# Four gate projections moved between the retention's steps, one search operation moved to GpSimd, and the retention's PSUM copies moved to ScalarE

## The chip, the cores and the metric

The kernel runs on one core of a Trainium2 chip. The metric is the device time of one execution in microseconds (us); lower is better. The core's engines run their own instruction streams in order and wait for one another through semaphores: PE (TensorE, matmuls; PEld is its weight load), DVE (VectorE), ACT (ScalarE), POOL (GpSimd) and SP (SyncE, here the queue that issues most DMAs).

## The reference, cut to what matters

The program is two layers of a hybrid decoder trunk for 1024 tokens of width 1024. The change lies in the first layer, whose input projection feeds two head groups:

```python
h = rms_norm(x, pre_norm[0])
(aq, ak, av, ag, iq, ik, iw, bq, bk, bv, bg) = split_columns(h @ w_in, EVEN_WIDTHS)
a = dsa_attention(aq, ak, av, iq, ik, iw)      # 256 best keys of each row, then softmax over those
a = a * jax.nn.silu(ag)                        # the selected-key gate, 512 columns
r = head_group_norm(retention(rotary(bq), rotary(bk) * 64 ** -0.5, bv))   # 8 chunks of 128, a state carried along
r = r * jax.nn.silu(bg)
x = x + rms_norm(concatenate([a, r]) @ w_out, post_norm[0])
```

`dsa_attention` finds for each query row the 256 keys with the highest index score. `retention` works chunk by chunk: the product inside the chunk, plus the state from the earlier chunks. Every projection is computed to float32 accuracy from a high and a low part, as three matmuls (low x high, high x low, high x high).

## The kernel before

**Search.** For the rows' blocks 2 to 7, `emit_threshold` (L521) finds the 256th score of every row by bisection over the score's upper 15 and lower 16 bits: 31 rounds, each of two chains of three blocks. In a chain, `count` counts the keys below the candidate, on ACT for blocks 7, 6 and 3 (L516) and on DVE for 2, 5 and 4 (L519). Then three operations on 128x3 numbers form the next candidate: `alt` (L535, the next lower candidate, which needs only the old one), `flag` (L536, compares the counts) and `cand` (L537, picks). All three are on DVE. Masks follow (`emit_mask`, L594 to L606).

**Retention.** `retention(p)`, for p = 0 and 1, handles two heads each. It loads weights, projects q and k (`pbqk`, turned by `rope_pairs`, L639 to L644, on DVE straight from PSUM), transposes them (`btq`, `btk`), projects v (`pbv`, copied out by ACT, L693), and then goes through 8 chunk steps: scores `bs`, `bsT` (L717, DVE), a state `bstate`, the output `bo`, and in each step 12 matmuls of its own gate `pbg`. The output leaves PSUM through DVE (L752, 128x256), followed by the statistics (L755, L756) and, later, the normalization (L770).

**Gates.** `gate_t` makes x times a sigmoid from a PSUM tile: a tanh on ACT (L622) and one operation on DVE (L623), both reading PSUM. `A_gate(p)` loads 128 columns of weights and computes two PSUM tiles `pag` of 8 steps (24 matmuls of 128x512) each, then writes the gate out to DRAM; it is read back transposed by head when the attention is combined. It has one call for each p from 0 to 3: 64 steps, 192 matmuls in all.

**Staging.** The search and both retentions are emitted together. Then come A_v(0), A_gate(0), A_qk(0), with the rest of retention 1 and the masks woven in, and then the attention units `units_A(0)` to `units_A(3)`, into whose steps a fill of further projections is spread evenly: 48, 80, 48 and 16 steps. The order on each engine is then set by the tile framework's scheduler from what it expects of the program as emitted, with data dependences and buffers kept.

**Buffers.** PSUM tiles of the tag `pj` (`pbqk`, `pbv`, `pbg`, `pag`, `pav`, `paq`, `pak`) share 2 buffers; so a third tile waits until the first is read out. High and low weight tiles (`whi`, `wlo`) have 6 buffers each, raw ones 4. `split_hl` (L244) makes them: a cast (on ACT, L248, or on POOL, L250), then the low part on POOL (L251). In the units, POOL also prepares the padded queries `zq` (L417) that the score matmuls L412 read.

Of the kernel before, what the change touches and what calls it, by code (L numbers as in the profile page):

```python
# [21 lines left out]
P = 128  # L22
# [123 lines left out]
def tile_hybrid_decoder(ctx: ExitStack, tc, x, positions, pre_norm, post_norm, w_in_even, w_out_even, w_in_odd,  # L146
# [374 lines left out]
    def emit_threshold():  # L521
# [4 lines left out]
        def bisect(bits, unsigned):  # L526
            for g in range(len(CHAINS)):
                V.memset(cand[:, cs_[g]], 2.0 ** (bits - 1) - 0.5)
            for b in range(bits - 1, -1, -1):
                for g, chain in enumerate(CHAINS):  # L530
                    s = cs_[g]
                    for q in chain:
                        c = col[q]
                        count(q, keys[q].bitcast(U16) if unsigned else keys[q], cand[:, c:c + 1], cnt[:, c:c + 1])
                    V.tensor_scalar(alt[:, s], cand[:, s], 2.0 ** (b - 1), None, op0=ALU.subtract)  # L535
                    V.tensor_tensor(flag[:, s], cnt[:, s], need[:, s], op=ALU.is_le)  # L536
                    V.scalar_tensor_tensor(cand[:, s], flag[:, s], 2.0 ** b, alt[:, s], op0=ALU.mult, op1=ALU.add)  # L537
# [96 lines left out]
    def rope_pairs(dst, src, tmp, cos, sin, nsin, half):  # L634
# [9 lines left out]
        V.tensor_tensor(dst, t1, t2, op=ALU.add)  # L644


    new_keys()
# [4 lines left out]
    def retention(p):  # L652
# [72 lines left out]
        for n in range(NB):  # L725
# [25 lines left out]
            rr = r[n // 4][:, n % 4, :]  # L751
            V.tensor_copy(rr.rearrange("p (h t) -> p h t", t=P), po[:, :, 0:P])  # L752
            st6 = small("bst", (P, 2, 6))
# [33 lines left out]

    def until(gen, val):
        for z in gen:
            if z == val:  # L790
                return

    until(B[0], 2)
    for k in range(20):
        if k >= 3:
            next(B[0], 0)
        next(B[1], 0)
    drain(B[0])
    until(B[1], 2)
    if dbg and upto == 3:  # L800
# [138 lines left out]

    def A_gate(p):  # L940
        w = load_w(w_in_even[0], [(AG + P * p, P)], "wag", hi_eng=G)
        for half in range(2):
            pp = pst("pag", "pj")
            yield from proj_t(pp, w, hT, 0, P, half)
            gate_out(pp, p * P, half)


# [92 lines left out]
    todo = chain(*(emit_mask(q) for q in (6, 7, 4, 5, 2, 3)))  # L1040
    for i, _ in enumerate(chain(A_v(0), A_gate(0), A_qk(0))):
        if i % 4 == 3 and i >= 12:
# [4 lines left out]
    outE = OutProj(w_out_even[0], pg1, pg2, 4, pg_raw=pg2)  # L1047
    fill = chain(A_qk(1), A_gate(1), A_v(2), A_qk(2), A_gate(2), A_qk(3), A_gate(3))
    pipe.run(units_A(0), islice(fill, 48), 48)
    pipe.run(units_A(1), islice(fill, 80), 80)  # L1050
    pipe.run(units_A(2), fill, 48)
    pipe.run(units_A(3), outE.first(2), 16)
# [422 lines left out]
```

## Time and profile before

| | us |
|---|---|
| median of 3 runs | 1304.21 (1302.02 to 1307.22) |
| the profiled execution | 1303.41 |
| its span in the trace | 1301.6 |
| PE busy | 1246.0 (96%) |
| PEld busy | 1029.2 (79%) |
| DVE busy | 800.5 (62%) |
| ACT busy | 682.6 (52%) |
| POOL busy | 411.5 (32%) |

Busy times are of the whole span; stages differ. In the trace the search runs from about 94 to 257 us, the retentions from about 60 to 271, the masks to 302, the attention units from about 330 to 600. A PE that is "busy" is not at its peak rate; the profile also gives the clock that the throttle granted it in a stretch.

### The profile page before, as it was taken

The numbers are of one execution on the slowest core, as the hardware profiler recorded it, in microseconds if no ns is written. First come the engines' busy times: TensorE is split into PE (matmuls) and PEld (weight loads), VectorE is DVE, ScalarE is ACT, GpSimd is POOL, SyncE is SP. The second block draws the span as 40 slices with busy tenths as digits, with TensorE's granted clock in tenths as the row PEclk, the third lists the DMA queues.
The fourth block names the chain that finished last, engine by engine and source line by source line (L and its number), as shares of the span: only waits on it lengthen the run. The fifth ranks groups of instructions, "written<-read, shape, count | busy, mean of one in ns | idle before, by whom it ended". The sixth has DMA issues, their size and how long they took to land.

```text
span 1301.6 us, 20092 instructions
## 1 busy us (share of the span) xinstructions
PE 1246.0 (96%) x7138; PEld 1029.2 (79%) x7138; DVE 800.5 (62%) x2020; ACT 682.6 (52%) x1510; POOL 411.5 (32%) x626
## 2 busy tenths in 40 slices
PE   7999989999999999889999999999999899999998
PEld 4788778798779877667887888889888777777786
DVE  6499999994654436484433344533654888887522
ACT  5578759602532424454545454554655677776421
POOL 4302232245251241444331233212322520435330
PEclk9999999999999999899999999999999999999999
DMA  5201111114121131225441113121322420232531
GB/s 192 57 25 34 33 34 57 34 26 121 29 71 32 34 89 40 79 89 184 148 121 42 49 49 90 58 60 42 122 65 89 110 53 30 75 97 66 187 125 65
DMA packets 92052, 97.70 MB, mean 75 GB/s; under 512 B 8118, under 2 KB 74448, under 8 KB 91952
## 3 DMA queue, kind: packets, MB, share of 16 engines
q1 hardware_dynamic: 87696, 82.39, 20.8%
q0 software_dynamic: 3968, 12.99, 3.6%
q8 instruction: 56, 0.92, 0.3%
q10 hardware_dynamic: 288, 1.05, 0.2%
q14 instruction: 44, 0.36, 0.1%
HBM read 68.74 MB, written 24.77 MB: 72 GB/s over the span
## 4 chain that ended last, share of the span: by engine, by line
PE 75%; DVE 13%; issue 4%; ACT 4%; POOL 4%; DMA 0%; POOLq 0%; DVEq 0%; ACTq 0%
PE tp L309 6%; PE bank L1009 5%; PE So L847 4%; PE So L848 4%; PE So L849 4%; DVE tj L519 3%; PE S L412 3%; PE S L411 3%; PE co L1176 2%; PE S L1419 1%; PE pav L301 1%; PE pav L303 1%; PE pav L302 1%; PE S L1421 1%; PE S L1420 1%
## 5 line engine op out<-in xcount | busy, mean ns | idle before, releaser
L1026 ACT ACTIVATE ae<-ae,nmx 128x128 f32<-128x128 f32 (+7 forms) x128 | 99.2, 776 | 90.1 <-DVE nmx L1024 89.6
L516 ACT ACTIVATE aj<-keys,tk_cand 128x1024 bf16<-128x1024 int16 (+5 forms) x96 | 93.2, 971 | 37.9 <-DVE tk_cand L537 14.9
L309 PE MATMUL tp<-cs,ae 128*128 128x128 f32 x576 | 89.3, 284 | 5.4 <-DVE pT L995 3.7
L309 PEld LDWEIGHTS tp<-cs,ae 128*128 128x128 f32 x576 | 68.7, 144 | 28.3 <-issue 9.3
L847 PE MATMUL So<-woh,mixl 128*128 128x512 f32 x224 | 87.7, 391 | 0.0
L849 PE MATMUL So<-woh,mixh 128*128 128x512 f32 x224 | 87.5, 391 | 0.0
L848 PE MATMUL So<-wol,mixh 128*128 128x512 f32 x224 | 87.5, 390 | 0.0
L1024 DVE CUSTOM_DVE_ANT_0 ce<-S,cmask 128x128 f32<-128x128 f32 (+7 forms) x64 | 48.2, 754 | 54.2 <-PE S L412 53.6
L519 DVE TENSOR_SCALAR_CACHE_REDUCE tj<-keys,tk_cand 128x384 bf16<-128x384 int16 (+5 forms) x96 | 79.9, 833 | 1.3
L1026 ACT ACTIVATE ce<-ce,nmx 128x128 f32<-128x128 f32 (+7 forms) x64 | 49.7, 776 | 53.0 <-DVE nmx L1024 52.7
L993 ACT COPY pT<-tp 128x384 f32<-128x384 f32 (+1 forms) x80 | 43.0, 538 | 54.4 <-PE tp L309 47.7
L995 DVE COPY pT<-tp 128x512 f32<-128x512 f32 (+1 forms) x80 | 50.7, 633 | 25.7 <-PE tp L309 22.8
L417 POOL CAST zq<-cqs 64x128 fp32r<-64x128 f32 x64 | 19.4, 304 | 146.9 <-PE S L412 143.3
L417 POOL CAST zq<-aqs 64x128 fp32r<-64x128 f32 x64 | 20.2, 316 | 129.7 <-PE S L412 127.1
L973 DVE TENSOR_SCALAR ae<-ae,ars 128x128 f32<-128x128 f32 (+7 forms) x96 | 58.4, 609 | 2.2
L1024 DVE CUSTOM_DVE_ANT_0 ae<-S,cmask,nrq 128x128 f32<-128x128 f32 (+3 forms) x64 | 51.4, 812 | 10.1 <-PE S L1421 8.3
L251 POOL TENSOR_TENSOR mixl<-mixr,mixh 128x512 fp32r<-128x512 f32 x32 | 41.5, 1306 | 35.3 <-ACT mixh L248 33.6
L412 PE MATMUL S<-akl,zq 128*128 128x512 f32 (+2 forms) x96 | 34.0, 365 | 17.2 <-POOL zq L417 17.2
L847 PEld LDWEIGHTS So<-woh,mixl 128*128 128x128 f32 x224 | 42.1, 188 | 9.3 <-issue 0.8
L848 PEld LDWEIGHTS So<-wol,mixh 128*128 128x128 f32 x224 | 42.1, 188 | 8.6
L849 PEld LDWEIGHTS So<-woh,mixh 128*128 128x128 f32 x224 | 42.1, 188 | 8.5
L329 ACT ACTIVATE junk<-So 128x512 bf16<-128x512 f32 x24 | 14.2, 593 | 56.0 <-PE So L849 42.2
(427 smaller groups left out, 4067.9 us busy)
## 6 DMA issues: line engine op xcount, KB each, us to landing
mixr<-mixT SPq DMA_DIRECT2D x32, 256.0 KB, 3.2
gT<-gate SPq DMA_DIRECT2D x24, 256.0 KB, 2.1
waqkr<-in_w_in_even_dram SPq DMA_DIRECT2D x32, 128.0 KB, 2.5
gin<-gT SPq DMA_DIRECT2D x32, 128.0 KB, 2.4
mixT<-gin SPq DMA_DIRECT2D x32, 128.0 KB, 1.8
wor<-in_w_out_even_dram SPq DMA_DIRECT2D x8, 512.0 KB, 4.0
xr<-in_x_dram POOLq DMA_DIRECT2D x8, 512.0 KB, 3.9
x1d<-xr SPq DMA_DIRECT2D x8, 512.0 KB, 3.3
```

The source lines that it names most:

```text
L309: nc.tensor.transpose(dst[:, k * P:(k + 1) * P], s, ident)
L412: nc.tensor.matmul(S[:, c:c + w], b, kl[:, c:c + w], start=False, stop=True)
L516: A.activation(aj[:, 0:n], src, AF.Sign, scale=-1.0, bias=edge, accum_out=dst)
L519: V.tensor_scalar(aj[:, 0:n], src, edge, None, op0=ALU.is_lt, op1=ALU.add, accum_out=dst)
L847: nc.tensor.matmul(dst, ml[k][:, bs], hi, start=(k == 0), stop=False)
L848: nc.tensor.matmul(dst, mh[k][:, bs], lo, start=False, stop=False)
L849: nc.tensor.matmul(dst, mh[k][:, bs], hi, start=False, stop=(k == kc - 1))
L973: V.tensor_scalar(e, e, rs, None, op0=ALU.mult)
L995: V.tensor_copy(pts[m][:, r, 0:n], tp[:, 0:n])
L1009: nc.tensor.matmul(bank[hp, o:o + wd], vp[:, kb, hp], pT[:, h, c:c + wd], start=(n == 0 or j == 0 and n == 1), stop=(n == len(jobs) - 1 or ...
L1024: V.tensor_tensor_reduce(out=e[:, 0:n], in0=S[:, 0:n], in1=mask, scale=scale, scalar=3.4e38, op0=ALU.add, op1=ALU.min, accum_out=nmx)
L1026: A.activation(e[:, 0:n], e[:, 0:n], AF.Exp, scale=-1.0, bias=nmx, accum_out=rsum)
```

## The change

Three things are done. `alt` goes from DVE to GpSimd. The retention's output copy goes from DVE to ScalarE. And `A_gate` is defined before the retention, loads its weights 128 columns wide (two raw tiles of four row blocks in place of four half-used tiles of two), and its 64 steps are drained between the steps of the retentions (`until` and the loop of 20), where they were before in front of A_qk(0) (16 steps) and in the fills of units 0, 1 and 2 (16 steps each).

```diff
@@ emit_threshold
-                    V.tensor_scalar(alt[:, s], cand[:, s], 2.0 ** (b - 1), None, op0=ALU.subtract)
+                    G.tensor_scalar(alt[:, s], cand[:, s], 2.0 ** (b - 1), None, op0=ALU.subtract)
@@ ahead of retention; the old A_gate, behind A_v, is deleted
+    def A_gate(p):
+        w = load_w(w_in_even[0], [(AG + P * p, P)], "wag", width=P, hi_eng=G)
+        for half in range(2):
+            pp = pst("pag", "pj")
+            yield from proj_t(pp, w, hT, 0, P, half)
+            gate_out(pp, p * P, half)
@@ retention, chunk step
-            V.tensor_copy(rr.rearrange("p (h t) -> p h t", t=P), po[:, :, 0:P])
+            A.copy(rr.rearrange("p (h t) -> p h t", t=P), po[:, :, 0:P])
@@ behind B = [retention(p) for p in range(2)]
-    def until(gen, val):
+    gates = chain(*(A_gate(p) for p in range(4)))
+
+    def until(gen, val, steps):
         for z in gen:
+            drain(islice(gates, steps))
             if z == val:
                 return
 
-    until(B[0], 2)
+    until(B[0], 2, 1)
     for k in range(20):
         if k >= 3:
             next(B[0], 0)
         next(B[1], 0)
+        drain(islice(gates, 2))
     drain(B[0])
-    until(B[1], 2)
+    until(B[1], 2, 2)
+    drain(gates)
@@ behind emit_threshold
-    for i, _ in enumerate(chain(A_v(0), A_gate(0), A_qk(0))):
+    for i, _ in enumerate(chain(A_v(0), A_qk(0))):
@@
-    fill = chain(A_qk(1), A_gate(1), A_v(2), A_qk(2), A_gate(2), A_qk(3), A_gate(3))
-    pipe.run(units_A(0), islice(fill, 48), 48)
-    pipe.run(units_A(1), islice(fill, 80), 80)
-    pipe.run(units_A(2), fill, 48)
+    fill = chain(A_qk(1), A_v(2), A_qk(2), A_qk(3))
+    pipe.run(units_A(0), islice(fill, 32), 32)
+    pipe.run(units_A(1), islice(fill, 64), 64)
+    pipe.run(units_A(2), fill, 32)
```

In the changed file the retention's lines have numbers that are 7 higher (L717 is L724 there, L755 is L762).

The first place is VectorE's stream in the chunk steps of retention 0, in the middle of the search. Before:

```order
L535 TENSOR_SCALAR tk_alt<-tk_cand 128x3
L519 TENSOR_SCALAR tj_795,tk_cnt<-keys_793,tk_cand 128x768
L535 TENSOR_SCALAR tk_alt<-tk_cand 128x3
L519 TENSOR_SCALAR tj_795,tk_cnt<-keys_793,tk_cand 128x640
L752 COPY br_1358<-bo_1457 128x256
L717 TENSOR_TENSOR bsT_1473<-bs_1470,cb_797 128x256
L755 BN_STATS bst_1465<-br_1358 128x6 x2
L756 BN_AGGR bmv_1360<-bst_1465 128x2
```

And the changed kernel's:

```order
L536 TENSOR_TENSOR tk_flag<-tk_cnt,tk_need 128x3
L537 SCALAR_TENSOR_TENSOR tk_cand<-tk_flag,tk_alt 128x3
L519 TENSOR_SCALAR tj_795,tk_cnt<-keys_793,tk_cand 128x768
L519 TENSOR_SCALAR tj_795,tk_cnt<-keys_793,tk_cand 128x640
L762 BN_STATS bst_1498<-br_1424 128x6 x2
L763 BN_AGGR bmv_1426<-bst_1498 128x2
L623 SCALAR_TENSOR_TENSOR bg_1427<-bg_1427,pbg_1443 128x512
L763 BN_AGGR bmv_1426<-bst_1498 128x2
L724 TENSOR_TENSOR bsT_1509<-bs_1506,cb_797 128x256
```

The lines L535 and L752 are gone from this stream, and the search's other operations stand closer together.

The second place is GpSimd's stream around the weights of retention 0's gate (`wbgl`), in the same part of the search. Before:

```order
L677 TENSOR_TENSOR bqk_839<-bqk_839,cb_797 128x4x128
L251 TENSOR_TENSOR wbgl_1343<-wbgr_1344,wbgh_1342 128x256 x2
L251 TENSOR_TENSOR wbgl_1351<-wbgr_1352,wbgh_1350 128x256 x2
L251 TENSOR_TENSOR wbqkl_1638<-wbqkr_1639,wbqkh_1637 128x256 x2
L251 TENSOR_TENSOR wbqkl_1647<-wbqkr_1648,wbqkh_1646 128x256 x2
```

And the changed kernel's:

```order
L535 TENSOR_SCALAR tk_alt<-tk_cand 128x3 x9
L251 TENSOR_TENSOR wbgl_1393<-wbgr_1394,wbgh_1392 128x256 x2
L251 TENSOR_TENSOR wbgl_1401<-wbgr_1402,wbgh_1400 128x256 x2
L251 TENSOR_TENSOR wbgl_1409<-wbgr_1410,wbgh_1408 128x256 x2
L250 CAST wagh_1623<-wagr_1625 128x128 x4
L251 TENSOR_TENSOR wbgl_1417<-wbgr_1418,wbgh_1416 128x256
L251 TENSOR_TENSOR wagl_1624<-wagr_1625,wagh_1623 128x128
L251 TENSOR_TENSOR wbgl_1417<-wbgr_1418,wbgh_1416 128x256
L251 TENSOR_TENSOR wagl_1624<-wagr_1625,wagh_1623 128x128 x3
L535 TENSOR_SCALAR tk_alt<-tk_cand 128x3 x6
```

The search's `alt` now stands in one queue with the splits of the weights, here nine of it ahead of a run of 16 splits and six behind.

The third place is TensorE's stream in a chunk step of retention 0. Before:

```order
L742 MATMUL bo_1457<-bstate_1426,bqx_837 128x128
L715 MATMUL bs_1470<-bqT_835,bkT_836 128x128 x2
L734 MATMUL bu_1475<-bv_1102,bqk_838 64x128 x2
L289 MATMUL pbg_1444<-hTh_129,wbgl_1343 128x512
L290 MATMUL pbg_1444<-hTl_137,wbgh_1342 128x512
```

And the changed kernel's:

```order
L749 MATMUL bo_1490<-bstate_1459,bqx_837 128x128
L289 MATMUL pag_1301<-hTh_130,wagl_907 128x512
L290 MATMUL pag_1301<-hTl_138,wagh_906 128x512
L291 MATMUL pag_1301<-hTh_130,wagh_906 128x512
L722 MATMUL bs_1506<-bqT_835,bkT_836 128x128 x2
L741 MATMUL bu_1511<-bv_1139,bqk_838 64x128 x2
```

One step of a gate, three matmuls, now stands in each chunk step, and its tile `pag` keeps one of the two `pj` buffers over eight such steps.

## Rows read from the trace of the kernel before

**Rows 1.** The page, part 1: busy time, share of span, instructions.

```profile
PE 1246.0 (96%) x7138; PEld 1029.2 (79%) x7138; DVE 800.5 (62%) x2020; ACT 682.6 (52%) x1510; POOL 411.5 (32%) x626
```

**Rows 2.** Busy times by stretch: length, engines, granted clock, DMA share, GB/s.

```profile
100.00:270.00 170.00, 161.18 (x1079) 138.66 (x1077) 161.44 (x564) 118.43 (x254) 48.89 (x58) 0.99 0.14 37
182.00:257.00 75.00, 69.63 (x488) 61.46 (x488) 72.12 (x262) 58.45 (x123) 17.40 (x23) 0.98 0.14 40
330.00:600.00 270.00, 249.82 (x1496) 202.55 (x1497) 151.09 (x356) 117.48 (x242) 88.42 (x173) 0.96 0.21 61
```

**Rows 3.** PE's waits, 100 to 270 us: total us, times, longest us.

```profile
PE btq L309 <- DVE bqk L644: 2.1, 1, 2.1
PE bo L740 <- DVE br L752: 1.7, 2, 1.3
PE pbv L301 <- DVE rp L643: 1.0, 1, 1.0
```

**Rows 4.** Stretch behind the wait at 193.25: columns as in rows 2.

```profile
193.80:197.20 3.40, 3.40 (x18) 3.40 (x17) 3.29 (x14) 3.30 (x7) 1.27 (x1) 0.50 0.02 5
```

**Rows 5.** DVE's groups by form, 94 to 258 us: busy us, mean ns, idle before.

```profile
L535 DVE TENSOR_SCALAR tk_alt<-tk_cand 128x3 f32<-128x3 f32 x60 | 11.0, 193 | 0.0
L770 DVE TENSOR_SCALAR br<-br,bmv,brs 128x128 f32<-128x128 f32 x21 | 6.0, 341 | 4.2 <-POOL brs L242 4.2
L755 DVE BATCH_NORM_STATS2 bst<-br 128x6 f32<-128x128 f32 x24 | 5.7, 280 | 0.0
L717 DVE TENSOR_TENSOR bsT<-bs,cb 128x256 f32<-128x256 f32 x14 | 5.7, 416 | 0.0
L752 DVE COPY br<-bo 128x256 f32<-128x256 f32 x12 | 5.0, 419 | 0.0
L639 DVE TENSOR_TENSOR rp<-pbqk,tabB 128x512 f32<-128x512 f32 x6 | 4.1, 681 | 0.0
L623 DVE SCALAR_TENSOR_TENSOR bg<-bg,pbg 128x512 f32<-128x512 f32 x6 | 4.0, 663 | 0.6 <-ACT bg L622 0.6
L642 DVE TENSOR_TENSOR rp<-pbqk,tabB 128x256 f32<-128x256 f32 x6 | 2.5, 412 | 0.0
```

**Rows 6.** DVE's timeline at two places: start us, us.

```profile
138.06 0.17 DVE L535 TENSOR_SCALAR tk_alt<-tk_cand 128x3 f32<-128x3 f32 x1
138.18 0.88 DVE L519 TENSOR_SCALAR_CACHE_REDUCE tj<-keys,tk_cand 128x640 bf16<-128x640 int16 x1
...
206.94 0.70 DVE L536 TENSOR_TENSOR tk_flag<-tk_cnt,tk_need 128x3 f32<-128x3 f32 x1
207.67 0.66 DVE L537 SCALAR_TENSOR_TENSOR tk_cand<-tk_flag,tk_alt 128x3 f32<-128x3 f32 x1
```

**Rows 7.** POOL's timeline beside the two later rows of that.

```profile
206.36 3.38 POOL L251 TENSOR_TENSOR wbgl<-wbgr,wbgh 128x256 fp32r<-128x256 f32 x4
```

**Rows 8.** POOL's waits, 100 to 270 us: total us, times, longest us.

```profile
POOL wbgl L251 <- ACT wbgh L248: 28.1, 2, 15.2
```

**Rows 9.** ACT's groups by form, 60 to 330 us: busy us, mean ns.

```profile
L516 ACT ACTIVATE aj<-keys,tk_cand 128x1024 bf16<-128x1024 int16 x16 | 18.4, 1150 | 11.8 <-DVE tk_cand L537 8.2 <-DVE tk_need L569 2.5 <-DVE tk_flag L536 0.5
...
L693 ACT COPY bv<-pbv 128x256 f32<-128x256 f32 x16 | 5.6, 351 | 0.0
L622 ACT ACTIVATE bg<-pbg 128x512 f32<-128x512 f32 x8 | 4.7, 584 | 15.4 <-PE pbg L291 15.4
```

**Rows 10.** Tile `pag` alone, the first gate's stretch: PE, PEld, DVE, ACT, clock.

```profile
294.00:307.00 13.00, 11.68 (x48) 8.81 (x48) 0.69 (x1) 0.60 (x1) 1.00 0.32 86
```

**Rows 11.** PE's largest wait from 328 to 600 us.

```profile
PE S L412 <- POOL zq L417: 17.2, 6, 5.9
```

**Rows 12.** PE's timeline where unit 2 begins.

```profile
477.00 0.53 PE L412 MATMUL S<-akl,zq 128*128 128x256 f32 x1 [2.55 <-POOL zq L417]
```

**Rows 13.** POOL's groups by form, 318 to 560 us: busy us, mean ns.

```profile
L251 POOL TENSOR_TENSOR wagl<-wagr,wagh 128x128 fp32r<-128x128 f32 x24 | 10.8, 468 | 0.0
...
L250 POOL CAST wagh<-wagr 128x128 fp32r<-128x128 f32 x24 | 6.4, 296 | 11.6 <-PE pak L291 10.7 <-POOL zq L417 0.9
```

More of the change, by code (lines that the diff above doesn't have):

```diff
@@ L938, in A_v @@
                 A.activation(vs[i][:, b:b + 2, :], pp.rearrange("p (b i c) -> p b i c", b=2, i=2)[:, :, i, :], AF.Copy, scale=0.5)
[L940 to L945, printed above, removed]
     def pair_units(p, front, vp, row, grow, pages, merge=False):
```

## The prediction

> **What bounds the kernel now.** I read the page's busy shares first: PE is busy for 1246.0 of 1301.6 us [rows 1], so no more than 55.6 us of the span is PE idle time, and a change that leaves the matmuls as they are can only win there or from the clock. Next I read busy times by stretch. From 100 to 270 us, where search and retentions run, PE is busy for 161.18 of 170 us and DVE for 161.44 of 170 [rows 2]: two engines are nearly full, and PE idles 8.8 us. From 330 to 600 us, the attention units, PE idles 270 - 249.8 = 20.2 us, while DVE is only busy for 151 of 270 [rows 2]. PE's waits in the first stretch name DVE: 2.1 us for the rope's sum, 1.7 for the output copy L752, 1.0 for the rope's PSUM reads [rows 3]. Behind the 2.1 us wait PE runs 3.4 us at a granted clock of 0.50, the lower of its two levels [rows 4], which costs half of that, 1.7 us. So the change works on the stretch where DVE makes PE wait, and what can be had there is 8.8 + 1.7 = 10.5 us.
>
> The sum is made against the profiled execution's 1303.41 us, 0.8 us under the median of the runs, 1304.21.
>
> **The matmuls that move.** The 192 matmuls of the gates stay as they are, 11.7 us for each of the four gates [rows 10], some 47 us in all. They leave the stretch ahead of the units and three fills and enter the retentions. By themselves they cost or win nothing. What they win is time: they give PE work on which DVE has little to do (one operation of 0.66 us a tile [rows 5]).
>
> **What DVE is relieved of.** In the built order, between the first and the last `cand` (L537), DVE loses 60 `alt`, 12 output copies, 6 `bsT` and 8 `bst` (five chunk steps of retention 1 now stand behind the search's end) and gains two operations of L623. An `alt` lasts 193 ns by its group [rows 5], but in the timeline the next operation starts 0.12 us after it [rows 6]; operations overlap, so I count 0.1: 6 us. The copies are 12 x 0.42 = 5.0 us, `bsT` 6 x 0.42 = 2.5, `bst` 8 x 0.28 = 2.2, and the gates take back 1.3 [rows 5]: together 14 us of about 160.
>
> It is not spread evenly. In the search's second half, which in before is 182 to 257 us, PE idles 75 - 69.6 = 5.4 us and DVE 2.9 [rows 2]. There the order loses 32 `alt` (3.2 us), 6 copies (2.5), 3 `bsT` (1.2) and 2 `bst` (0.6), but takes in three gate operations (2.0) and seven more normalizations of L770 (7 x 0.34 = 2.4) [rows 5]: net 3 us. Of the 5.4 us, 3 come back; of the 3.4 in the first half, where the other 11 us of relief lie, all. **Term 1: -6 us** (0 to -8.8). The slow stretch at 193 us goes if its wait falls to a part; I count half of 1.7: **-0.8** (0 to -1.7).
>
> **Copies on ACT.** 16 copies of 128x256 from PSUM, 0.35 us each by the row of the same shape [rows 9], 5.6 us; ACT is busy for 118 of 170 us [rows 2] and has room. A copy can stand behind a count of 1.15 us [rows 9], but it holds an output buffer of which there are two, so it is hidden by the next chunk step (12 matmuls of 0.24 us, 2.9 us, by [rows 10]). Zero; if that cover were gone, 16 x 0.5 = 8 us, which I hold unlikely.
>
> **The buffers of tag `pj`.** This is the change's price. A `pag` tile now lives over eight steps with other work between, and so the other projections have one buffer left in place of two. In before, a `pbqk` tile's readout has the whole next tile to hide behind, 48 matmuls. In the changed order it has only what stands between: mostly two or three gate steps, 6 to 9 matmuls, 1.5 to 2.2 us [rows 10], or one step, 0.7. The readout takes 0.68 + 0.41 + 0.41 = 1.5 us for the rope, 0.58 + 0.66 = 1.25 for a gate [rows 5, 9], 0.35 for a copy on ACT, and up to 1.15 of queue ahead [rows 9]. I count 28 such places. Each is between 0 (an idle engine) and about 0.5 (1.5 + 1.15 against 2.2); I take 0.15, nearer to zero, since DVE and ACT wait in order and mostly stand ready: **term 2: +4 us** (0 to +14). The trace of before has no interleaved tile; its 1.0 us of `pbv` behind the rope [rows 3] shows that even a wide cover can fail.
>
> On this the Trainium skill, Perfetto Trace Analysis, section Matmuls, speaks against the change: independent matmul groups should rotate through different PSUM banks, so that one group's readout overlaps the next one's matmuls. No run so far shows its price; taken at its word the 28 readouts would stand uncovered, and the sum would rise by 10 us, to 1313.
>
> **POOL's queue.** `alt` needs only the old candidate, so on POOL it runs beside the counts; its result is due a count later, 0.88 us or more [rows 6]. But POOL works in order, and the stretch's queue is full of weight splits that wait: `wbgl` alone for 28.1 us in two waits, up to 15.2 [rows 8], until PE lets go of weight buffers. In the changed order nine `alt` stand ahead of one run of 16 splits and six behind; the run lasts 8 x 0.85 (3.38 for four [rows 7]) + 4 x 0.30 + 4 x 0.47 [rows 13] = 9.8 us. If it starts late, `cand` waits for `alt`, everything on DVE stands behind `cand`, and PE behind the rope. Three or four such runs lie in the search. The scheduler has put the `alt` where they fit by its own plan, and DVE has 14 us less to do; I take **+2 us** (0 to +16).
>
> There is a second effect. At 206.94 `flag` and `cand`, 128x3, last 0.70 and 0.66 us [rows 6], beside a run of POOL splits from 206.36 [rows 7]. POOL is busy for 48.9 us of the stretch [rows 2]; it gains 32 gate splits (16 x 0.30 + 16 x 0.47 = 12.3 us [rows 13]) and 62 `alt`. If small DVE operations suffer in proportion, and some ten lost half a microsecond each in before, that is 5 x 12.3 / 48.9 = 1.3: **+1 us**.
>
> The Trainium skill, Perfetto Trace Analysis, section Optimizing Scalar/DVE Operations, says that GpSimd and DVE share a read port of SBUF, and that moving work between them might not help. The slow `flag` agrees with it. By that rule the 6 us of `alt` would not be won, and the sum would be 1307.
>
> **The units.** Fills of 48, 80 and 48 steps become 32, 64 and 32. Unit 3 runs with 16. PE's largest wait there is for `zq` on POOL, 17.2 us in 6 times [rows 11], where splits for the fill stand ahead of it. At unit 2, 4 casts and 4 splits of `wag` (4 x 0.30 + 4 x 0.47 = 3.1 us [rows 13]) leave POOL's run in front of `zq`, and one split of another weight takes their place; of the 2.55 us wait [rows 12] I let about 2 go. At unit 0 splits twice as wide come in for them, +1. Thinner fill can uncover softmax chains: DVE has 151 us for what becomes 250 - 35 = 215 of PE, still no bound. **Term 3: -1 us** (-4 to +5).
>
> **Sum:** -6 - 0.8 + 4 + 2 + 1 - 1 = -0.8, so 1302.6; I say **1302 us**, about no change.
>
> **The rivals.**
> - *The stretch becomes purely PE-bound* (faster). The readouts and `alt` hide, as DVE's relief of 14 us against 8.8 us of idle PE allows: -8.8 - 1.7 - 1 gives 1292. For it: all of PE's large waits in the stretch are for DVE. Against it: in the second half only 3 us are taken off DVE, and a buffer is taken away at the same time.
> - *POOL's queue holds the search* (slower). Three runs of 9.8 us, each holding `cand` by half, 15 us of DVE time, on an engine that was 95% busy; the relief of 14 us is eaten, PE stays as late as before, and the readouts' 4 us and some of the queue come on top: 1303.4 + 10 = 1313. It decides from about 13 us of DVE waiting for POOL on.
> - *Single buffer at full price*: 28 x 0.5 = 14 in place of 4 gives 1312.
> - *The move only shifts the loss* (the fills are missed in the units): +5 in place of -1, 1308, within no change. That the scheduler would put the gates back is excluded by the built order.
>
> **How the numbers follow.** A measurement of this kernel tells about 0.5%, 6.5 us, from no change. Chances: no change as forecast 0.44 (with 1308 and the 1307 of the shared port in it), the PE-bound stretch 0.30, slower 0.26 (POOL 0.15, buffers 0.11). The forecast's own range is 1297.7 to 1310. The range for 8 in 10 reaches from 1291, all of the idle and slow time gone, to 1315, just beyond the two slower cases.
>
> **What would show it.** Right: PE's idle time from 100 us to the end of retention 1 falls from 8.8 to between 5 and 10 with the waits now many and short, at the first matmul of `pbqk`, `pbv`, `pbg` and `pag`, for DVE's rope, L623 or ACT's copies; the wait for L752 is gone; DVE waits for `alt` a few times behind weight splits. The units' idle time stays near 20 us. Wrong: PE waits below 3 us in the stretch (the buffers cost nothing), waits of `cand` for `alt` of over 10 us, or units that differ by more than 5 us. What would upset the sum is a change of the granted clock elsewhere, as a slow stretch of 3.4 us costs 1.7.

## The result and the profile after

The changed kernel takes 1320.57 us (median of 4 runs, 1319.26 to 1322.71); the kernel before, on the same chip, 1305.51 us (4 runs). The ratio is 1.012 with a 95% interval of 1.0093 to 1.0148: some 15 us slower. The time lies above the predicted 1302 us and above the whole range, 1291 to 1315. The two profiled spans are 1320.9 and 1301.6 us, 19.3 us apart, so the profiled pair lies a little further apart than the medians (15.1 us).

The page's busy times of the changed kernel, beside [rows 1]:

```profile
PE 1256.1 (95%) x7138; PEld 1030.9 (78%) x7138; DVE 799.8 (61%) x1942; ACT 691.3 (52%) x1526; POOL 418.3 (32%) x688
```

PE does the same 7138 matmuls and is busy 10 us longer, which already says that part of the loss is a lower clock or wider spacing, not idle time alone. DVE has 78 instructions fewer and is off by 0.7 us only.

To place the loss, I cut both traces at the same points of the program: **R**, from the first matmul of retention 0 (`pbqk`) to the first `pav`, holds search and retentions; **U**, from there to the first matmul into the tile `So`, holds the attention units; then the rest. Busy times by stretch (length, engines, granted clock, DMA share, GB/s), of before:

```profile
62.10:270.80 208.70, 199.66 (x1327) 172.66 (x1325) 196.48 (x632) 148.30 (x302) 53.24 (x63) 0.99 0.14 37
270.80:597.20 326.40, 305.41 (x1841) 252.49 (x1840) 188.94 (x428) 126.70 (x261) 117.52 (x223) 0.97 0.22 64
597.20:1295.20 698.00, 686.33 (x3729) 566.94 (x3728) 377.01 (x881) 372.88 (x876) 215.51 (x302) 1.00 0.29 87
```

and of after:

```profile
62.00:326.80 264.80, 250.37 (x1517) 209.64 (x1516) 218.89 (x610) 160.64 (x327) 87.43 (x185) 0.98 0.17 47
326.80:616.90 290.10, 265.98 (x1649) 218.76 (x1648) 166.41 (x373) 123.30 (x254) 89.35 (x160) 0.95 0.19 56
616.90:1314.50 697.60, 686.39 (x3729) 566.65 (x3728) 376.50 (x881) 373.31 (x877) 215.96 (x302) 1.00 0.29 87
```

The rest is the same to 0.4 us. The gates' 192 matmuls left U and entered R; in before, counted from the start of each to the start of the next, they fill 45.2 us. Taking these 45.2 us along:

| part | before | after | moved work | net | of it idle PE | of it clock | left over |
|---|---|---|---|---|---|---|---|
| R | 208.7 | 264.8 | +45.2 | +10.9 | +5.4 | +3.4 | +2.1 |
| U | 326.4 | 290.1 | -45.2 | +8.9 | +3.1 | +5.1 | +0.7 |

Idle PE is length less PE's busy time (R 9.0 to 14.4, U 21.0 to 24.1 us). The clock's part is half the added time at the lower level (a granted clock of 0.50): 3.4 to 10.2 us in R, 20.5 to 30.7 us in U. It is a little too high where PE also idles in such a stretch, which then counts twice.

**R.** PE's waits in after (what PE waited for: us in total, times, longest):

```profile
PE pbv L301 <- DVE gate L623: 3.2, 1, 3.2
PE pbqk L301 <- DVE tk_flag L536: 2.7, 1, 2.7
PE pbv L301 <- DVE rp L643: 2.4, 2, 1.8
PE pag L289 <- DVE tk_flag L536: 2.1, 1, 2.1
PE pbqk L301 <- DVE tk_cand L537: 2.0, 1, 2.0
...
```

The waits of before for `btq` and `bo` [rows 3] and for `btr`, 5.3 us together, are gone. Every wait now stands at the first matmul of a projection that needs a `pj` buffer: 14.2 us in ten waits, against 2.5 us in three in before. Four of the ten, of 2.0 to 3.2 us, make 10.0 of the 14.2. Where the releaser reads `tk_flag` or `tk_cand`, the profile names the operation that happened to end last; in the stream of VectorE it is the rope's readout that holds the buffer (start, duration, line, operation):

```profile
102.19 0.61 DVE L519 TENSOR_SCALAR_CACHE_REDUCE tj<-keys,tk_cand 128x384 bf16<-128x384 int16 x1
...
103.19 1.01 DVE L519 TENSOR_SCALAR_CACHE_REDUCE tj<-keys,tk_cand 128x768 bf16<-128x768 int16 x1
...
104.25 0.88 DVE L519 TENSOR_SCALAR_CACHE_REDUCE tj<-keys,tk_cand 128x640 bf16<-128x640 int16 x1
...
105.05 0.69 DVE L639 TENSOR_TENSOR rp<-pbqk,tabB 128x512 f32<-128x512 f32 x1
105.66 0.41 DVE L642 TENSOR_TENSOR rp<-pbqk,tabB 128x256 f32<-128x256 f32 x1
105.99 0.41 DVE L643 TENSOR_TENSOR rp<-pbqk,tabB 128x256 f32<-128x256 f32 x1
```

and in TensorE's, the last matmul of the tile, the last of the cover, and the next tile's first:

```profile
101.77 0.29 PE L303 MATMUL pbqk<-wbqkh,hTh 128*128 128x256 f32 x1
...
103.49 0.40 PE L290 MATMUL pag<-hTl,wagh 128*128 128x512 f32 x1
106.55 0.36 PE L301 MATMUL pbqk<-wbqkh,hTl 128*128 128x256 f32 x1 [2.66 <-DVE tk_flag L536]
```

The tile is complete at 102.06. Its readout needs 1.35 us, but begins at 105.05, since three counts of the search and their small operations stand ahead of it on VectorE; the cover, transposes and six gate matmuls, is used up at 103.9. Three such waits have a stretch at the lower level (1.2 GHz) around their end, at 200.8, 211.0 and 262.2 us; the last of them:

```profile
262.20:265.60 3.40, 2.98 (x14) 2.99 (x15) 3.40 (x6) 0.00 (x0) 0.00 (x0) 0.50 0.41 157
```

This one goes with the 3.2 us wait, in which a gate's readout (0.69 us at 261.87) stood behind two operations of the masks, a scan of 2.29 us and a sum of 1.13 us.

**U.** The waits for `zq` fell from 17.2 us [rows 11] to 12.5; those of the transposes `tp` for `pT`, a copy on VectorE behind the normalizations, grew. In before and in after:

```profile
PE tp L309 <- DVE pT L995: 2.9, 1, 2.9
```

```profile
PE S L412 <- POOL zq L417: 12.5, 5, 3.3
PE tp L309 <- DVE pT L1000: 7.6, 2, 5.6
PE pav L301 <- DVE gate L623: 1.6, 1, 1.6
...
```

The 1.6 us are one more wait for a `pj` buffer, behind the last gate. The 5.6 us are at unit 1. On VectorE, then on GpSimd, then on TensorE:

```profile
463.61 0.48 DVE L978 TENSOR_SCALAR ae<-ae,ars 128x384 f32<-128x384 f32 x1
464.58 6.82 DVE L978 TENSOR_SCALAR ae<-ae,ars 128x512 f32<-128x512 f32 x1
471.31 0.68 DVE L1000 COPY pT<-tp 128x512 f32<-128x512 f32 x1
```

```profile
464.88 0.74 POOL L250 CAST waqkh<-waqkr 128x256 fp32r<-128x256 f32 x2
465.58 1.42 POOL L251 TENSOR_TENSOR waqkl<-waqkr,waqkh 128x256 fp32r<-128x256 f32 x2
...
469.71 1.40 POOL L251 TENSOR_TENSOR waqkl<-waqkr,waqkh 128x256 fp32r<-128x256 f32 x2
```

```profile
472.05 1.76 PE L309 MATMUL tp<-cs,ae 128*128 128x128 f32 x7 [5.57 <-DVE pT L1000]
```

A normalization of 128x512, of a kind that elsewhere in this kernel lasts 0.49 us (median), lasts 6.82 us, as long as GpSimd works through the split of `A_qk(2)`'s weights without a pause. (`x2` stands for two instructions in a row.) Around the wait's end the granted clock is 0.50 for 6.8 us:

```profile
470.40:477.20 6.80, 5.15 (x16) 4.52 (x17) 2.44 (x4) 0.48 (x1) 0.77 (x3) 0.50 0.23 70
```

In before the longest of the 64 normalizations, of up to 1024 columns, lasts 2.62 us, and it too lies beside GpSimd splits, longer ones of another weight:

```profile
572.99 2.62 DVE L973 TENSOR_SCALAR ae<-ae,ars 128x512 f32<-128x512 f32 x1
```

```profile
570.54 7.26 POOL L251 TENSOR_TENSOR wol<-wor,woh 128x1024 fp32r<-128x1024 f32 x3 [0.17 <-POOL zq L417]
```

### The profile page after: what moved, and what is told of

It reads as the page before. It is cut to its first block, busy times and chain, and to the rows that moved or that the text cites. A ratio compares the mean times of both kernels' runs of the same rounds, so it can differ in the third digit from the quotient of the medians.

```text
span 1320.9 us, 20118 instructions
## 1 busy us (share of the span) xinstructions
PE 1256.1 (95%) x7138; PEld 1030.9 (78%) x7138; DVE 799.8 (61%) x1942; ACT 691.3 (52%) x1526; POOL 418.3 (32%) x688
## 4 chain that ended last, share of the span: by engine, by line
PE 73%; DVE 15%; POOL 4%; ACT 4%; issue 3%; DMA 1%; SPq 0%; DVEq 0%; POOLq 0%; ACTq 0%
PE tp L309 5%; PE bank L1014 5%; PE So L859 4%; PE So L860 4%; PE So L861 4%; DVE tj L519 4%; PE S L412 3%; PE S L411 3%; PE co L1181 2%; PE S L1424 1%; DVE ae L978 1%; PE S L1426 1%; PE S L1425 1%; PE pcg L291 1%; PE pcg L290 1%
## 5 line engine op out<-in xcount | busy, mean ns | idle before, releaser
L309 PEld LDWEIGHTS tp<-cs,ae 128*128 128x128 f32 x576 | 68.2, 144 | 33.0 <-DVE pT L1000 11.5
L978 DVE TENSOR_SCALAR ae<-ae,ars 128x128 f32<-128x128 f32 (+7 forms) x96 | 65.8, 687 | 2.0
L535 POOL TENSOR_SCALAR tk_alt<-tk_cand 128x3 f32<-128x3 f32 x62 | 15.3, 249 | 108.4 <-DVE tk_cand L537 92.6
L412 PE MATMUL S<-akl,zq 128*128 128x512 f32 (+2 forms) x96 | 35.7, 384 | 12.5 <-POOL zq L417 12.5
```

The source lines that it names most:

```text
L309: nc.tensor.transpose(dst[:, k * P:(k + 1) * P], s, ident)
L412: nc.tensor.matmul(S[:, c:c + w], b, kl[:, c:c + w], start=False, stop=True)
L978: V.tensor_scalar(e, e, rs, None, op0=ALU.mult)
```

## Experiments

Theories at the start. **A**: in R the gates' tiles take one of two `pj` buffers, so a readout that stands behind search work on in-order VectorE is no longer covered. **B**: what costs is the interleaving itself (PE switches between tiles), whatever VectorE does. **C**: `alt` on GpSimd or the copies on ScalarE cost it. For U, **D**: GpSimd's unbroken split holds the normalization. All ratios are to the kernel before on the same chip. The expectations were written run by run and use letters of their own: S, and later "theory B", there stand for the lost buffer, L for VectorE's lateness, Q, M and C for a part of the change, P for D, F for the units' thinner fill, and B2 for the short covers alone.

### Parts one and two alone: `alt`, and the copies

```diff
-                    V.tensor_scalar(alt[:, s], cand[:, s], 2.0 ** (b - 1), None, op0=ALU.subtract)
+                    G.tensor_scalar(alt[:, s], cand[:, s], 2.0 ** (b - 1), None, op0=ALU.subtract)
```

> Part 1 alone: the kernel before with only alt (L535) on GpSimd. Theory S (single buffer): the loss of about 15 us comes from the gates' PSUM tiles that keep one of two pj buffers, so this part alone is harmless: DVE has about 6 us less in the search, PE idles less; 1299 to 1306. Rival Q (GpSimd's queue): alt behind waiting splits holds the search; 1308 or more, with waits of cand for alt of over 5 us. Rival M (shared port): no gain at all, 1305, small DVE operations lengthened.

1303.08 us, 0.9992 (0.9979 to 1.0004). The 60 operations take 13.9 us on GpSimd, and no `cand` waits for them. VectorE is relieved of them, and nothing measurable comes of that: in R, PE's idle time goes from 9.0 to 7.8 us, the low clock from 3.4 to 6.8. The waits for `btq` (2.0 us), `bo` (1.1) and `btr` (1.3) are still there.

```diff
-            V.tensor_copy(rr.rearrange("p (h t) -> p h t", t=P), po[:, :, 0:P])
+            A.copy(rr.rearrange("p (h t) -> p h t", t=P), po[:, :, 0:P])
```

> Part 2 alone: the kernel before with only the retention's output copy on ScalarE. Theory S: 1301 to 1307, DVE relieved by 5 us in the search. Rival C (the copies): in the changed kernel DVE's statistics waited 11.0 us for these copies in 7 waits, because they stand behind ScalarE's counts; if that is what costs, this kernel is slower, 1309 to 1313, with those waits in it.

1307.92 us, 1.0036 (1.0021 to 1.0051): between the two forecasts. R is 213.0 us, 4.3 longer (idle 9.0 to 11.5, low clock 3.4 to 10.2). Two of its waits:

```profile
PE pbqk L301 <- DVE tk_flag L536: 2.9, 1, 2.9
PE bo L740 <- ACT br L752: 1.3, 1, 1.3
```

The copies are not free: the wait for `br` [rows 3] did not vanish but became one for ScalarE. In the changed kernel VectorE waits 11.0 us in seven times for the copy.

### Part three alone: the gates

The changed kernel with `alt` and the copies back on VectorE (the two lines above, reversed).

> Part 3 alone: the changed kernel with alt and the copies back on VectorE. Theory S: it keeps the whole loss or more, 1319 to 1328, since DVE has about 11 us more in the search and the readouts are as bare as before. Rivals Q and C: without their part the loss falls below half, under 1312.

1326.16 us, 1.0172 (1.0151 to 1.0193). C is out: the moved gates make the whole loss and more, and in their company the other two parts take some microseconds off (the medians say 5.6, the profiled spans 1.7). R is 265.0 us against 264.8 in the changed kernel, with 15.4 us of idle PE against 14.4, and the waits for `btq`, `br` and `btr` are gone here too, though VectorE still has all its work: it is the moved gates that cover them. U is 290.3 us, with a normalization of 6.79 us in the same place.

### Whole tiles in place of interleaved ones

The gates are given out eight steps at a time, so that a `pag` tile is not open across other work:

```diff
+    def give(steps):
+        owed[0] += steps
+        if owed[0] >= 8:
+            owed[0] -= 8
+            drain(islice(gates, 8))
...
-            drain(islice(gates, steps))
+            give(steps)
```

> The changed kernel with the gates' 64 steps handed out in whole tiles (8 steps, 24 matmuls in a row, as soon as 8 are owed) in place of 1 or 2 at a time. The same matmuls move to the same stage; only a gate tile no longer lies over other tiles. Theory S: PE's waits at the first matmul of pbqk, pbv and pag in the retentions fall from 14 to under 8 us, two or three of the half-speed stretches go, and the interleaving overhead goes; the retention part gets 8 to 12 us shorter: 1307 to 1313. Rival F (the loss is the units' thinner fill): unchanged, 1318 to 1322.

1324.95 us, 1.016 (1.0131 to 1.019): missed. R is 268.4 us with 20.8 us of idle PE. The largest wait, on TensorE, with the first of the operations on VectorE that end it, and the first reading of the gate tile that is complete at 206.55, on ScalarE:

```profile
222.27 0.55 PE L301 MATMUL pbqk<-wbqkh,hTl 128*128 128x256 f32 x1 [7.36 <-DVE tk_flag L536]
```

```profile
220.78 0.69 DVE L639 TENSOR_TENSOR rp<-pbqk,tabB 128x512 f32<-128x512 f32 x1
```

```profile
231.67 0.57 ACT L622 ACTIVATE gate<-pag 128x512 f32<-128x512 f32 x1
```

The projection before it ended at 214.0; five counts and their small operations, from 215.60 to 220.78, stood ahead of its rope. The other buffer was not free either: the whole gate tile lay in it unread for 25 us, behind ScalarE's counts. So whole tiles did not give the second buffer back, and the work that was to cover readouts had been ordered elsewhere. It speaks for A, with ScalarE's queue beside VectorE's, but was not the clean undoing that I meant it to be.

### The gates' tiles in another bank

```diff
-            pp = pst("pag", "pj")
+            pp = pst("pag", "t")
```

> The changed kernel with the gates' tile pag in the PSUM tag t (2 buffers, otherwise for the transposes and bu) in place of pj; so pbqk, pbv and pbg have both pj buffers again, and the gates are still interleaved step by step. Theory B (the lost buffer): the waits of PE at the first matmul of pbqk, pbv and pag in the retentions go from 14 us to under 8, the retention part (first pbqk to first pav, 264.9 us in the changed kernel) gets 7 to 11 us shorter; 1309 to 1314. Rival L (VectorE runs behind, since the search is packed between the ropes whatever the buffers): the waits move to the transposes or stay; retention part within 4 us; 1317 to 1322.

1320.70 us, 1.0127 (1.0102 to 1.0152), as the rival had it. The `pj` waits are gone and others stand there:

```profile
PE btk L309 <- DVE bqx L678: 12.1, 4, 7.5
PE btr L309 <- DVE gate L623: 3.4, 2, 2.7
```

The transposes now share the tag `t` with the gates and wait just as `pbqk` did. The buffer that is taken makes the place, the readouts behind it make the wait. (In the profiled execution the granted clock is 0.95 nearly throughout where the others show 1.00, so I compare only its waits.)

### Shorter and fewer search steps

If search work ahead of the readouts is what costs, taking it away must take R's loss away. First each count on VectorE covers a quarter of its keys, with limits to match (the selected keys are then others), in the kernel before (`e6_short_b`) and after (`e6_short_a`):

```diff
-            V.tensor_scalar(aj[:, 0:n], src, edge, None, op0=ALU.is_lt, op1=ALU.add, accum_out=dst)
+            V.tensor_scalar(aj[:, 0:n // 4], src[:, 0:n // 4], edge, None, op0=ALU.is_lt, op1=ALU.add, accum_out=dst)
...
```

> The kernel before, with VectorE's counts over the first quarter of the keys only (blocks 2, 4 and 5; the limits scaled with it), so that VectorE has some 50 us less in the search; the selection is then not the reference's. It is the base for the next run: PE's waits on VectorE in the retentions should nearly go, 1294 to 1301.

> The changed kernel with the same quarter counts. Against the run before: theory B (the lost buffer alone) keeps the difference, 13 to 18 us, since the gate tiles still hold a buffer. Rival L (VectorE's lateness) shrinks it to what lies in the attention units and the interleaving, 8 to 11 us, with PE's waits in the retentions under 4 us in both.

1292.29 us, 0.9905 (0.9877 to 0.9932), and 1310.99 us, 1.005 (1.0029 to 1.0072). Before loses nearly all its idle PE in R (1.1 us left), after keeps 7.8; the distance, 18.7 us, stays (both a little outside their forecasts). That looks like B, but VectorE's waits in `e6_short_a` take the point away:

```profile
DVE tk_flag L536 <- ACT aj L516: 25.7, 25, 3.9
```

ScalarE's counts, which were not shortened, now set the search's pace, and VectorE's readouts stand behind operations that wait for them. So this pair decided nothing. The same counts with whole tiles (`e10_whole_short`, the edits of `e4_whole` and `e6_short_a`) fell to the same thing (its third gate tile, complete at 199.3, is first read at 220.9):

> Whole gate tiles (as in e4_whole) and quarter counts on VectorE (as in e6_short_a; the selection is not the reference's). If VectorE's lateness is what made whole tiles wait (7.4 us at one place), the retention part is that of e6_short_b and the gates' 43 us, 196 + 43 = 239 to 242, PE's waits there under 3 us. If whole tiles wait for something else: over 246.

1312.59 us, 1.0059 (1.0039 to 1.008), R 257.2 us with 12.1 idle: missed.

Then only three of the search's 15 and three of its 16 rounds are run, on all engines alike (again with other keys selected):

```diff
-            for b in range(bits - 1, -1, -1):
+            for b in range(bits - 1, bits - 4, -1):
```

> The kernel before with 3 of the 15 and 3 of the 16 rounds of the search (the selection is not the reference's). Base for the next run: with hardly any search on VectorE and ScalarE, PE's idle time in the retentions should be under 2 us, as in e6_short_b (1.1), and the retention part 195 to 197 us.

> The changed kernel with the same 3 and 3 rounds; TensorE's order and the buffers with their short covers (0.7 to 2.3 us at some 30 places) stay. Theory A (search steps that stand ahead of a readout on VectorE's in-order stream, and are no longer covered): without them the readouts fit the covers, PE's waits for pbqk, pbv and pag fall from 14 us to under 4, the retention part is 196 + 45 + 3 = 240 to 246 us. Rival B2 (the short covers alone): 6 us or more of such waits stay, 248 us or more.

Before with it: 1299.24 us, 0.9948 (0.9933 to 0.9964); after with it: 1310.19 us, 1.0044 (1.0028 to 1.006). Both missed their forecast for R: the base by 7 to 9 us (203.7, with 6.1 us of idle PE in place of under 2), and so the other with it, 254.3. R by stretch, of `e12_few_b` and of `e12_few_a`:

```profile
62.00:265.70 203.70, 197.64 (x1326) 172.42 (x1324) 141.15 (x364) 74.52 (x152) 53.23 (x63) 0.99 0.14 38
```

```profile
62.40:316.70 254.30, 247.29 (x1518) 206.94 (x1517) 148.17 (x360) 85.49 (x177) 81.31 (x135) 0.99 0.18 49
```

and PE's waits in the latter:

```profile
PE pbqk L301 <- DVE tk_flag L536: 2.7, 1, 2.7
...
PE pbv L301 <- DVE rp L643: 1.0, 1, 1.0
PE pbv L301 <- ACT bv L700: 0.9, 1, 0.9
PE pag L289 <- DVE rp L643: 0.9, 1, 0.9
```

The covers are nearly those of the changed kernel (about a hundred of the 3164 matmuls of R and U stand in another order). Still, R's loss falls from 10.9 to 254.3 - 203.7 - 45.2 = 5.4 us, idle PE differs by 0.9 us (7.0 against 6.1) and the low clock by nothing (3.4 each). The waits for a `pj` buffer are 5.7 us, over the 4 that A allowed and under the 6 of the rival; against the base of each they add 2.9 us here and 11.7 in the changed kernel. The one of over 2 us is that of 106.55, and it lies in the three rounds that remain; those at 200.7 and 262.6 are gone, and that at 210.9 fell from 2.1 to 0.9. That is A: a lone buffer costs where search work stands ahead of its readout. What stays, 4.5 us with neither idle time nor clock in it, is spacing: in the changed kernel the tile `pag` takes 54.25 us of PE in R, in before 48.11 in U, and given out in whole tiles (`e4_whole`) 45.48 in R, with the same 192 matmuls. After, before and `e4_whole`:

```profile
62.00:327.00 265.00, 54.25 (x192) 33.76 (x192) 4.78 (x7) 4.17 (x7) 0.98 0.17 47
```

```profile
270.80:597.20 326.40, 48.11 (x192) 34.75 (x192) 5.50 (x8) 4.77 (x8) 0.97 0.22 64
```

```profile
61.60:330.00 268.40, 45.48 (x192) 35.46 (x192) 4.75 (x7) 4.16 (x7) 0.97 0.17 48
```

Part of the difference is the half-speed stretches that fall on them. In `e4_whole` R is 268.4 - 208.7 - 45.2 = 14.5 us too long, and idle PE (11.8) and clock (5.1) account for all of it; in the interleaved kernels 2 us (the changed kernel) to 6 us (`e6_short_a` against `e6_short_b`) are left over. So B holds too, for 2 to 6 us; what in a change of tile costs PE that time was not told apart.

### The units: another order, and GpSimd relieved

```diff
-    fill = chain(A_qk(1), A_v(2), A_qk(2), A_qk(3))
+    fill = chain(A_qk(1), A_qk(2), A_v(2), A_qk(3))
```

> The changed kernel with the fill in the order A_qk(1), A_qk(2), A_v(2), A_qk(3), 32, 64 and 32 steps as before. In the changed kernel one normalization on VectorE (L978, 128x512) took 6.8 us at 464.6, as long as GpSimd worked without a pause on the weights of A_qk(2), PE waited 5.6 us for it, and a half-speed stretch of 6.8 us followed. Theory P (GpSimd's run holds the operation): with the run elsewhere no VectorE operation of the units is over 3 us, the units (first pav to first So, 290.1 us) get 6 to 9 us shorter, 1311 to 1315. Rival F (the thinner fill leaves the softmax chains bare): unchanged, 1318 to 1322.

1321.41 us, 1.0127 (1.0093 to 1.0161): missed. The split came earlier, met another normalization (128x384, 4.57 us at 463.7, PE idle for 2.99), and a `zq` wait grew from 1.2 to 3.1 us. It moved the collision, and told nothing of its cause. The direct test takes the split of `A_qk(2)` off GpSimd (high parts on ScalarE, low parts on VectorE), with TensorE's order left as it is:

```diff
-        w = load_w(w_in_even[0], [(AQ + P * p, P), (AK + P * p, P)], "waqk", hi_eng=G)
+        w = load_w(w_in_even[0], [(AQ + P * p, P), (AK + P * p, P)], "waqk", hi_eng=None if p == 2 else G, eng=V if p == 2 else G)
...
-                split_hl(hi[:, k, 0:tot], lo[:, k, 0:tot], raw[:, k, 0:tot], eng=G, hi_eng=hi_eng)
+                split_hl(hi[:, k, 0:tot], lo[:, k, 0:tot], raw[:, k, 0:tot], eng=eng, hi_eng=hi_eng)
```

> The changed kernel with the splits of A_qk(2)'s weights taken off GpSimd: high parts on ScalarE, low parts on VectorE. TensorE's order is the changed kernel's but for one matmul. Theory P (GpSimd's pauseless run holds VectorE's normalization): the 6.8 us normalization and the 5.6 us wait behind it are gone although VectorE has eight splits more, and the half-speed stretch of 6.8 us with them; the units 287 to 280 us in place of 290, total 1310 to 1317. Rival F (thin fill): a wait of the same size stays in that place, 1318 to 1324.

1310.21 us, 1.0055 (1.0034 to 1.0076); against the changed kernel 10.4 us less by the medians, 8.5 by the ratios. U, the operation in question, and PE's wait:

```profile
328.50:603.70 275.20, 258.60 (x1650) 212.87 (x1648) 163.74 (x381) 125.25 (x262) 81.31 (x144) 0.98 0.20 59
```

```profile
469.89 0.49 DVE L978 TENSOR_SCALAR ae<-ae,ars 128x512 f32<-128x512 f32 x1
```

```profile
PE tp L309 <- DVE pT L1000: 2.1, 1, 2.1
```

U is 14.9 us shorter (idle 24.1 to 16.6, low clock 30.7 to 10.2), more than the one collision, whose own share is the 5.6 us wait and up to 3.4 us of clock. A wait of 2.4 us for `zq` went with the same split, and other stretches at the lower level went though their waits stayed (3.2 us for `zq` at 381.6 had none behind it). D stands: without the run on GpSimd, none of these normalizations lasts over 2.83 us. The thinner fill, which is the same here, is not what cost: U is now 6.0 us less than 326.4 - 45.2. That relieving GpSimd also shortens U of the kernel before shows below.

### One gate, and versions that beat both

Only gate 0 moves; gates 1 to 3 stay in fills of 48, 80 and 48 steps, with `alt` and the copies as in the change:

```diff
+    gates = A_gate(0)
...
-    for i, _ in enumerate(chain(A_v(0), A_gate(0), A_qk(0))):
+    for i, _ in enumerate(chain(A_v(0), A_qk(0))):
```

> Only the first gate (16 of 64 steps) is moved between the retention's steps, gates 1 to 3 stay in the fills of 48, 80 and 48 steps; alt on GpSimd and the copies on ScalarE as in the changed kernel. If each moved gate costs alike (the retention part of the changed kernel is 11 us over the sum of what was there and what came, the units 9 us): 1307 to 1310. If the units' part needs the fill without gates: the units as before (first pav to first So 326.5 less the 11.3 us of the gate, 315), no VectorE operation there over 3 us, and 1304 to 1308.

1303.37 us, 0.9994 (0.9982 to 1.0005): neither gain nor loss, and under both forecasts. The gate costs 3.1 us in R (223.1 us less 208.7 and its 11.3) and spares 2.7 in U (312.4).

Since GpSimd is what the units wait for, in before as well [rows 11], I left the gates where they were, kept `alt` on GpSimd, and gave ScalarE the high parts of `waqk` and `wag`:

```diff
-        w = load_w(w_in_even[0], [(AQ + P * p, P), (AK + P * p, P)], "waqk", hi_eng=G)
+        w = load_w(w_in_even[0], [(AQ + P * p, P), (AK + P * p, P)], "waqk")
...
-        w = load_w(w_in_even[0], [(AG + P * p, P)], "wag", hi_eng=G)
+        w = load_w(w_in_even[0], [(AG + P * p, P)], "wag")
```

> A version that might beat both: the kernel before with alt on GpSimd, and the high parts of waqk and wag cast on ScalarE in place of GpSimd. GpSimd's runs ahead of zq, for which PE waits 17.2 us in the units, lose about a third; if no wait takes their place, 4 to 8 us faster than before, 1297 to 1301. Rival: ScalarE, in order, stands at these casts until TensorE lets go of the weight buffers, and the softmax behind it waits: 1305 to 1312.

1294.67 us, 0.9926 (0.9903 to 0.9949), U 316.9 us, and better than the forecast by some 2 us. Then in addition every other low part of the first layer's output weights on VectorE:

```diff
-                    split_hl(hi, lo, raw, eng=G, hi_eng=self.hi_eng)
+                    split_hl(hi, lo, raw, eng=V if k % 2 else G, hi_eng=self.hi_eng)
```

> A version that might beat e11_act (1294.7): that kernel, and every other low part of the first layer's output weights (wol) on VectorE in place of GpSimd. They stand ahead of zq in unit 3, where PE waits 5.9 us and two half-speed stretches of 3.4 us follow: 1288 to 1293 if that goes; 1294 to 1297 if VectorE only passes the wait on.

**1287.13 us, 0.9864 (0.9841 to 0.9887)**, the fastest here, just under its forecast. Its U, and PE's largest wait there:

```profile
271.10:580.70 309.60, 300.84 (x1841) 247.36 (x1840) 190.83 (x432) 143.38 (x321) 87.52 (x156) 0.99 0.23 67
```

```profile
PE S L412 <- POOL zq L417: 5.7, 4, 3.3
```

Idle PE in U fell from 21.0 to 8.8 us, the waits for `zq` from 17.2 us [rows 11] to 5.7, the low clock from 20.5 to 3.4. Gate 0 moved on top of it, with the copies on VectorE (the edits of `e13_out` and `e8_one`):

> The version before this one with the first gate between the retention's steps (as e8_one, but the copies on VectorE). If the copies on ScalarE were what cost in e8_one (3 us by e2_copy): the retention part is 2 to 4 us shorter than there and the total 1286 to 1292; if the single gate costs by its readouts: as e13_out or up to 4 us slower.

1292.15 us, 0.9903 (0.9873 to 0.9932), 5 us slower, just past the forecast: even one gate costs more in R (226.8 us, of which its matmuls are some 11) than it spares in U. The copies on ScalarE were not what cost in `e8_one`, where R was 223.1 us.

## Why the prediction was wrong, step by step

- **What bounds the kernel**: right. PE's idle time and clock made the difference, all in R and U.
- **Relief of VectorE (term 1, -6)**: the waits that it was to remove, for `btq`, `bo` and `btr`, are gone, 5.3 us, but not by the relief, so the size is luck. They are gone in `e3_gates` too, where VectorE is not relieved, and stand in `e1_alt`; the moved gates cover them. In the company of the gates the relief took 1.0 us of idle PE off R, and alone `alt` gave 0.9992 and the copies 1.0036.
- **The buffers of `pj` (term 2, +4)**: the step that failed in R. Their waits grew by 11.7 us, and 3.4 us of clock came with them. The kind of place (the first matmuls of `pbqk`, `pbv`, `pbg` and `pag`) and the durations of the readouts were right; the wrong part is "0.15, nearer to zero, since DVE and ACT wait in order and mostly stand ready". VectorE was 95% busy there [rows 2] (89% from 100 to 252 us in the changed kernel), and did not stand ready: a readout found three counts, 3.0 us with their small operations, ahead of it, or the masks' 3.4 us. The bound on the queue ahead, 1.15 us, took one operation where several stood, and the bound of 0.5 a place took the widest cover, 2.2 us, though covers of 0.7 are named beside it, which by the same sum leave 2.0 bare. Cutting the search to three rounds in each half took three quarters of the added waits away (`e12_few_a`). The upper end that I had worked out, +14, is near by its number but not by its make-up: not 28 places of 0.5 us but ten waits, four of them 2.0 to 3.2 us. The Trainium skill's rule (Perfetto Trace Analysis, section Matmuls), that independent groups of matmuls should rotate through different banks, gave 1313: nearer than my choice, and in R by the right mechanism.
- **Spacing of the interleaved matmuls**: not in the sum at all ("By themselves they cost or win nothing"); 2 us here, up to 6 in other interleaved runs, nothing measurable in whole tiles.
- **The clock (-0.8)**: wrong in sign. The slow stretch of before [rows 4] went, three others came: +3.4 in R.
- **The copies (0)**: alone they cost 0.36%, in company nothing that was told apart. "Hidden by the next chunk step" failed where a copy came late on ScalarE (PE waited 1.3 us for one in `e2_copy`).
- **GpSimd's queue (+2, up to +16)**: did not come. `cand` waited for GpSimd once, 0.5 us, and the rival that hung on it, 1313, did not come about; that its time is nearer to the measured one is chance.
- **GpSimd beside small VectorE operations (+1)**: nothing came of it in the search: from 94 to 258 us `flag` and `cand` take 24.7 us in before and 24.5 in `e1_alt`. So `alt` alone won nothing, as the paragraph on the shared port had it, but not because these operations grew longer; and its 1307 does not follow, since 6 us added to 1302.6 are 1308.6. I had priced the effect only on operations of 128x3, where [rows 6] showed it.
- **The units (term 3, -1)**: the step that failed in U, +8.9. Unit 2's `zq` wait fell from 2.55 [rows 12] to 1.22 us and unit 0's rose by 0.6, as said. What I left out is that shorter fills bring `A_qk(2)`'s split forward to where a normalization runs on VectorE. `e9_qk2` gave 8 to 10 us back by taking that split off GpSimd, of which the collision itself is 5.6 us of waiting and up to 3.4 of clock. "Units that differ by more than 5 us" was named as what would prove the sum wrong; it did.

Two terms thus missed, about half of the loss each (R +10.9, with 2 us of spacing in it, and U +8.9), and both in one direction: the first took a busy engine for a ready one, the second moved weight preparation on GpSimd without asking what VectorE does at its new time. The third, term 1, came out in size only because the gates covered the waits that the relief was to remove.

## What to carry to other kernels

Before a buffer is taken from a rotation, look at the stream of the engine that reads it out, and price the wait by all that the order puts ahead of the readout there, not by the readout; where that engine is nearly full, a step or two of work moved in between does not cover it. When a change moves weight preparation on GpSimd, look for the VectorE operations on the critical chain at the new time. Here the idle time to be won lay where PE waited for GpSimd, and spreading its splits over ScalarE and VectorE (with `alt` on GpSimd) won 1.4%, with no matmul moved.

## What the runs showed of the hardware

- An unbroken run of GpSimd casts and subtractions held one VectorE operation of 128x512 for 6.82 us in place of 0.49; in another order (`e7_order`) it held one of 128x384 for 4.57 us in place of 0.41; with the run gone the first lasted 0.49. Not every GpSimd instruction holds VectorE so: at 463.61, beside a split, one of 128x384 took 0.48 us. The Trainium skill, SBUF — State Buffer, section Who interferes with whom, says that a VectorE instruction in a two-port mode, which `tensor_scalar` can enter, contends with GpSimd: whoever issues first gets the port pair they share for the whole instruction, and the other fully blocks. Which mode these operations ran in no run shows. The trace agrees that VectorE blocks, and differs in how long: in before the operation of 2.62 us was held for about one GpSimd split of some 2.4 us, but in the changed kernel GpSimd's instructions are 0.4 us (casts) and 0.7 us (subtractions) long, and VectorE was held over the whole run of them, from 464.58 to 471.40. Why it did not come in between is not shown.
- Three of the four single buffer waits of about 2 us or more in R had at their end 3.4 us at a granted clock of 0.50; the one at 106.55, 2.66 us, had none. In `e12_few_a` and `e9_qk2` the wait at the same place, of the same length, did have one. What made the difference was not tested.
- Sixty operations of 128x3 taken from an engine that was 95% busy made no measurable difference.
